# Experts in chunks of 1024 columns, with a branch on TensorE by an expert's token count

## The chip, the cores and the metric

One NeuronCore of a Trainium2 chip runs the whole kernel. The metric is the device time of one execution in microseconds, as a median of several runs. TensorE (PE) multiplies matrices, VectorE (DVE) and ScalarE (ACT) work elementwise, GpSimd (POOL) does little here, and SyncE (SP) issues the loads of the weights from HBM.

## The reference

A trunk of two layers over 256 tokens with 1024 features, in float32. Layer 0 is attention and a dense SwiGLU, layer 1 a gated recurrence (HGRN2) and eight SwiGLU experts, of which each token uses two. The change lies in the experts alone:

```python
def moe_swiglu(u, w_router, w_gate, w_up, w_down):      # D 1024, 8 experts, D_FF_EXPERT 3584
    t = u.reshape(B * S, D)                             # 256 tokens
    logits = (t @ w_router).astype(F32)
    top_vals, top_idx = lax.top_k(logits, 2)
    top_w = jax.nn.softmax(top_vals, axis=-1)
    gates = jnp.sum(jax.nn.one_hot(top_idx, N_EXPERTS) * top_w[..., None], axis=1)
    for e in range(N_EXPERTS):
        y = swiglu(t, w_gate[e], w_up[e], w_down[e])    # (silu(t @ wg) * (t @ wu)) @ wd
        out = out + gates[:, e:e + 1] * y
```

With the inputs of this reference the numbers of tokens of experts 0 to 7 are 65, 69, 45, 58, 68, 76, 61 and 70 (worked out from the reference on a CPU; the second and third highest logits of a token are nowhere closer than 0.015).

## The kernel before

**Exact products in three passes.** Weights and rows are float32. `split` cuts each weight tile into two parts: ACT copies it to `w_hi` in float32r (the format that PE multiplies at full rate), and DVE subtracts that from the raw tile and writes the rest to `w_lo`. Rows are cut in the same way (`xgh` and `xgl`, or `hh` and `hl`). `mm3` (lines 100 to 103) then adds three products in one PSUM bank: high rows by `w_hi`, high rows by `w_lo`, low rows by `w_hi`. The rows are the stationary operand (`lhsT`), 512 weight columns stream.

**Experts.** Each expert has 128 slots for its tokens. `route` works out the votes (`sel`), each token's place in an expert's list (`place`) and its gate (`gw`); `one_hot` makes from `place` a matrix of tokens by slots, and `gather_pair` multiplies the tokens by it, for two experts at once (256 columns). `Job` is a chunk of 512 of an expert's 3584 hidden columns, seven to an expert: `gate` and `up` (two loads of 1 MB each, four conversions and four subtractions of 128x1024 each, 24 products each), `turn` (four transposes of `hm`, then `hh` and `hl`) and `down` (again 1 MB twice, 24 products, into two banks `py` that live over the expert). `run_jobs` puts the gate of the next chunk ahead of `turn`, and `up` ahead of `down`. After an expert's last chunk `scatter` multiplies `py` by the turned one-hot matrix, and DVE adds the result, times the gate, to the residual stream `h`. The first gate (`FirstJob.gate`) works on all 256 tokens, 48 products, so that PE has work while the tokens are routed.

**Order and queues.** SP's queue holds the loads in program order; each lands in one of `NRAW` = 14 buffers `raws` of 8 KB per partition, freed when DVE has subtracted. `w_hi` and `w_lo` have four buffers each (`subs`). The tile framework orders each engine's instructions; an instruction waits on semaphores for what it reads and for its buffer. At the end `values_load` reads the greatest token count into a register of each engine (line 1261), and a branch (line 1262) leaves out a block for slots 128 to 255, which these inputs don't need.

Of the kernel before, what the change touches and what calls it, by code (L numbers as in the profile page):

```python
# [8 lines left out]
F32 = mybir.dt.float32  # L9
# [17 lines left out]
NRAW = 14  # L27
NSUB = 4
STOP = None
# [10 lines left out]
def tile_trunk(  # L40
# [25 lines left out]
    subs = ctx.enter_context(tc.tile_pool(name="subs", bufs=NSUB))  # L66
# [3 lines left out]
    early = ExitStack()  # L70
    xts = early.enter_context(tc.tile_pool(name="xts", bufs=1))
# [62 lines left out]
    def col_steps(xh, xl, w, c0, ps):  # L134
        """steps, one per k-tile, of x @ w[:, c0:c0+256] into ps, token tile after token tile"""
# [15 lines left out]
    def row_steps(xh, xl, wv, ks, acc, first, last):  # L151
        """steps, one per k-tile and token tile, of x @ w (all 1024 columns) into acc[t][c]"""
# [13 lines left out]
    def row_tail(xh, xl, wv, k0, acc, last, kx=0, first=False, between=None):  # L166
        """two k-tiles of x @ w, token tile by token tile"""
# [11 lines left out]
    def weave(fill, main):  # L179
        """the steps of fill, with those of main after the given amounts of fill"""  # L180
# [12 lines left out]
    def table_fn(*a, **k):  # L193
        """an activation that needs its table: those keep their order"""
# [9 lines left out]
    def gain_tile(g, late):  # L204
        """a norm's gains on all partitions; loaded once the given 1 / rms is known"""
# [13 lines left out]
    GAIN_A = 32     # columns of the first norm's gains  # L219
# [11 lines left out]
    def turn_params(rows):  # L231
        """gains and lower-bound logits to columns"""
# [4 lines left out]
    def small_params(lam_in):  # L237
        """factors into the gains; lambda of the differential attention, negated, on every partition"""
# [15 lines left out]
    def root(ap):  # L254
        """ap ** -0.5: from its logarithm, then one step of Newton's to full accuracy"""
# [9 lines left out]
    def rsqrt_mean(ap, n, width):  # L265
        """(ap / n + eps) ** -0.5"""
# [3 lines left out]
    def rms(t):  # L270
        """1 / rms of the rows of h[t], the sum taken by halves"""
# [31 lines left out]
    def norm_T(hgs, gain, acc, into=None):  # L303
        """(h * gain)^T in two parts, and 1 / rms of the rows of h; after h += acc"""
# [775 lines left out]
    class Job:  # L1080
# [6 lines left out]
        def rows(self):  # L1087
            return [(*self.shared["xg"], self.es)]
# [247 lines left out]
```

## Time and profile before

| what | value |
|---|---|
| time, median of 3 runs | 1511.85 us (1510.98 to 1514.09) |
| span of the profiled execution | 1509.5 us |
| median less that span | 2.35 us |
| PE, DVE, ACT busy | 98%, 82%, 69% |
| HBM read | 427.41 MB |

The profiled execution's time is its span; what the runs' median has more lies around the span or is the difference of one execution from another. Busy shares are those of the whole span. The experts take it from about 495 us to 1503 us, and before that lie the layers that the change leaves alone.

### The profile page before, as it was taken

What the parts mean: (1) busy time and instruction counts of PE and PEld (TensorE: products, weight loads), DVE (VectorE), ACT (ScalarE), POOL (GpSimd) and SP (SyncE); (2) the same over time, 40 slices, a digit from 0 to 9 for tenths busy, and PEclk for the clock granted to TensorE, in tenths of its full rate; (3) what the DMA queues carried; (4) which work ended last, traced back from release to release, by engine and by line L of the source; (5) the groups of instructions that cost most, each with busy time, mean ns of one, the idle gap of its engine ahead of it and who ended that gap; (6) DMA issues with size and microseconds to landing.
All of it is one profiled execution on the core that took longest, in us unless ns stands there. A gap on an engine that the chain in (4) does not pass through costs nothing.

```text
span 1509.5 us, 20242 instructions
## 1 busy us (share of the span) xinstructions
PE 1476.0 (98%) x7573; PEld 1228.3 (81%) x7573; DVE 1243.6 (82%) x1474; ACT 1042.5 (69%) x1293; POOL 14.9 (1%) x32
## 2 busy tenths in 40 slices
PE   7999999999999999999999999999999999999997
PEld 6787899998888788888888878888777887887885
DVE  7775655566767899999899998898889889889886
ACT  6655544445656788878778877777777777777774
POOL 1000000000000000000000000000000000000000
PEclk9999999999999999999999999999999999999999
DMA  9933456555443499999999999999999999999970
GB/s 312 368 117 112 137 185 195 178 185 182 140 156 125 142 376 363 373 364 362 360 325 377 377 329 362 371 315 362 362 369 345 361 355 326 362 363 343 365 260 31
DMA packets 208683, 429.85 MB, mean 285 GB/s; under 512 B 7290, under 2 KB 58530, under 8 KB 208578
## 3 DMA queue, kind: packets, MB, share of 16 engines
q1 hardware_dynamic: 208082, 426.82, 80.2%
q0 software_dynamic: 496, 1.67, 0.4%
q8 instruction: 61, 1.00, 0.3%
q14 instruction: 44, 0.36, 0.1%
HBM read 427.41 MB, written 1.05 MB: 284 GB/s over the span
## 4 chain that ended last, share of the span: by engine, by line
PE 92%; DVE 3%; ACT 2%; issue 1%; DMA 1%; POOL 0%; SPq 0%; ACTq 0%; DVEq 0%; POOLq 0%
PE acc L102 17%; PE acc L101 17%; PE acc L103 16%; PE pj L103 8%; PE pj L102 8%; PE pj L101 8%; PE pj L342 3%; PE pj L344 3%; PE pj L343 3%; DVE w_lo L91 2%; PE tp L1116 1%; PE pj L759 1%; PE pj L760 1%; PE pj L761 1%; PE acc L1069 1%
## 5 line engine op out<-in xcount | busy, mean ns | idle before, releaser
L91 DVE TENSOR_TENSOR w_lo<-raw,w_hi 128x1024 fp32r<-128x1024 f32 x810 | 958.5, 1221 | 163.4 <-ACT w_hi L91 146.1
L91 ACT ACTIVATE w_hi<-raw 128x1024 fp32r<-128x1024 f32 x810 | 835.8, 1058 | 275.8 <-PE acc L103 101.9
L102 PE MATMUL acc<-w_lo,xgh 128*128 128x512 f32 x904 | 357.2, 395 | 0.9
L101 PE MATMUL acc<-w_hi,xgh 128*128 128x512 f32 x904 | 355.9, 394 | 1.0 <-ACT xgh L294 1.0
L103 PE MATMUL acc<-w_hi,xgl 128*128 128x512 f32 x904 | 353.1, 391 | 0.0
L102 PEld LDWEIGHTS acc<-w_lo,xgh 128*128 128x128 f32 x904 | 169.7, 188 | 50.3 <-DVE w_lo L91 14.5
L101 PEld LDWEIGHTS acc<-w_hi,xgh 128*128 128x128 f32 x904 | 169.8, 188 | 36.4 <-ACT xgh L294 1.2
L103 PEld LDWEIGHTS acc<-w_hi,xgl 128*128 128x128 f32 x904 | 169.7, 188 | 33.8
L102 PE MATMUL pj<-w_lo,hh 128*128 128x512 f32 x448 | 177.1, 395 | 0.3
L103 PE MATMUL pj<-w_hi,hl 128*128 128x512 f32 x448 | 174.6, 391 | 0.3
L101 PE MATMUL pj<-w_hi,hh 128*128 128x512 f32 x448 | 161.1, 391 | 2.2 <-ACT hh L1120 1.7
L101 PEld LDWEIGHTS pj<-w_hi,hh 128*128 128x128 f32 x448 | 84.1, 188 | 21.5 <-ACT hh L1120 2.7
L102 PEld LDWEIGHTS pj<-w_lo,hh 128*128 128x128 f32 x448 | 84.1, 188 | 18.2 <-DVE w_lo L91 1.6
L103 PEld LDWEIGHTS pj<-w_hi,hl 128*128 128x128 f32 x448 | 84.1, 188 | 17.5 <-DVE hl L1121 1.1
L342 PE MATMUL pj<-xh,w_hi 128*128 128x256 f32 x320 | 90.8, 284 | 0.6 <-DVE hm L676 0.6
L344 PE MATMUL pj<-xh,w_lo 128*128 128x256 f32 x320 | 90.6, 283 | 0.0
L343 PE MATMUL pj<-xl,w_hi 128*128 128x256 f32 x320 | 90.6, 283 | 0.0
L1106 ACT ACTIVATE sg<-acc 128x512 f32<-128x512 f32 x55 | 33.0, 599 | 46.7 <-PE acc L103 46.7
L342 PEld LDWEIGHTS pj<-xh,w_hi 128*128 128x128 f32 x320 | 61.4, 192 | 1.2 <-DVE hm L676 0.8
L343 PEld LDWEIGHTS pj<-xl,w_hi 128*128 128x128 f32 x320 | 61.4, 192 | 0.4
L344 PEld LDWEIGHTS pj<-xh,w_lo 128*128 128x128 f32 x320 | 61.4, 192 | 0.0
L1120 ACT ACTIVATE hh<-tp 128x512 fp32r<-128x512 f32 x56 | 33.3, 595 | 40.4 <-PE pj L102 33.2
(296 smaller groups left out, 1648.1 us busy)
## 6 DMA issues: line engine op xcount, KB each, us to landing
raw<-in_moe_w_gate_dram SPq DMA_DIRECT2D x112, 1024.0 KB, 7.1
raw<-in_moe_w_up_dram SPq DMA_DIRECT2D x112, 1024.0 KB, 7.6
raw<-in_moe_w_down_dram SPq DMA_DIRECT2D x110, 1024.0 KB, 7.4
raw<-in_ffn_w_gate_dram SPq DMA_DIRECT2D x22, 512.0 KB, 4.0
raw<-in_ffn_w_up_dram SPq DMA_DIRECT2D x22, 512.0 KB, 5.1
raw<-in_ffn_w_down_dram SPq DMA_DIRECT2D x11, 1024.0 KB, 4.9
raw<-in_hgrn_w_in_dram SPq DMA_DIRECT2D x10, 1024.0 KB, 5.7
raw<-in_attn_w_in_dram SPq DMA_DIRECT2D x16, 512.0 KB, 9.1
```

The source lines that it names most:

```text
L91: split.last = nc.scalar.activation(hi, view, AF.Copy), nc.vector.tensor_sub(lo, view, f32(hi))
L101: nc.tensor.matmul(ps, lhsT=xh, rhs=wh, start=first, stop=False, skip_group_check=chk)
L102: nc.tensor.matmul(ps, lhsT=xh, rhs=wl, start=False, stop=False, skip_group_check=chk)
L103: nc.tensor.matmul(ps, lhsT=xl, rhs=wh, start=False, stop=last, skip_group_check=chk)
L342: nc.tensor.matmul(o, lhsT=wh[:, i, j], rhs=xh[:, k], start=k == 0 and j == 0, stop=False, skip_group_check=True)
L343: nc.tensor.matmul(o, lhsT=wh[:, i, j], rhs=xl[:, k], start=False, stop=False, skip_group_check=True)
L344: nc.tensor.matmul(o, lhsT=wl[:, i, j], rhs=xh[:, k], start=False, stop=k == KT - 1, skip_group_check=True)
L759: nc.tensor.matmul(o, lhsT=wh[:, k], rhs=xh[:, k], start=first, stop=False, skip_group_check=True)
L760: nc.tensor.matmul(o, lhsT=wh[:, k], rhs=xl[:, k], start=False, stop=False, skip_group_check=True)
L761: nc.tensor.matmul(o, lhsT=wl[:, k], rhs=xh[:, k], start=False, stop=last, skip_group_check=True)
L1106: nc.scalar.activation(self.sg, ps, AF.Silu)
L1120: nc.scalar.activation(self.hh, ptv, AF.Copy)
```

## The change

The experts' code is written anew. These are its parts:

- A chunk has 1024 columns (the first of expert 0 and the last of every other have 512), and a chunk's weights come in `Group`s of one 1 MB load, one conversion and one subtraction of 128x2048. `w_hi` has three such buffers and `w_lo` two. `NRAW` is 11. A row of a load is 4 KB (gate, up) or 8 KB (down), where it was 2 KB or 4 KB.
- `route` also counts the tokens of each expert, and `value_load` reads the eight counts into registers of PE.
- Every group's products stand in a branch on PE. Above 64 tokens: the same 12 products. Up to 64 tokens: 8 products, whose stationary operand has 64 high rows and 64 low rows at once (the high and low part of a row lie side by side in `xg` and `hq`, and a slice with step 2 takes 64 of each). Rows 64 to 127 of the result are then the low rows' share.
- Behind a gate or an up of any expert ACT copies the bank to `low`. In `fold`, in a second branch on PE, experts of up to 64 tokens add rows 64 to 127 to rows 0 to 63 with a product by `lower`; the other experts jump over it.
- For experts of up to 64 tokens the one-hot matrices are other ones (`pick`, `even`, `twice`), and the transposes in `turn` multiply by a permutation `order`. The sharing of low rows on the way out is done by `scatter`, whose one-hot matrix has each token twice.

```diff
-NRAW = 14
+NRAW = 11
@@ route
+            if t == NT - 1:
+                pc = bank("tp")
+                for u in range(NT):
+                    nc.tensor.matmul(pc[:, 0:NE], lhsT=ones, rhs=sel[:, u], start=(u == 0), stop=(u == NT - 1))
+                nc.vector.tensor_copy(count, pc[:, 0:NE])
...
+                nc.vector.tensor_scalar(few, pc[:, 0:NE], float(HS), None, op0=ALU.is_le)
...
+                nc.vector.tensor_reduce(out=cmax_i, in_=count, axis=AX.X, op=ALU.max)
@@ Group
+        def split(self):
+            self.hi = parts.tile([P, 2048], F32R, name="w_hi", tag="w_hi", bufs=3)
+            self.lo = parts.tile([P, 2048], F32R, name="w_lo", tag="w_lo", bufs=2)
+            nc.scalar.activation(self.hi, self.raw, AF.Copy)
+            nc.vector.tensor_sub(self.lo, self.raw, f32(self.hi))
+        def __call__(self):
+            if self.n is None:
+                return self.arm(self.hi, self.lo, True)
+            with tc.If(self.n > HS) as cmp:
+                self.arm(self.hi, self.lo, True)
+            with cmp.Else():
+                self.arm(self.hi, self.lo, False)
...
+    def products(xq, wh, wl, ps, large, first, last):
+        if large:
+            xh, xl = xq[:, 0], xq[:, 1]
+            mm(ps, (xh, xh, xl), (wh, wl, wh), first, last)
+        else:
+            xs = xq.rearrange("p q s -> p (q s)")[:, 0:2 * P:2]
+            mm(ps, (xs, xs), (wh, wl), first, last)
@@ Job
+        def low(self, box):
...
+            for lo, ps in zip(box["low"], box["ps"]):
+                nc.scalar.activation(lo, ps, AF.Copy)
+        def fold(self, box):
...
+            with tc.If(self.n < HS + 1):
+                for lo, ps in zip(box["low"], box["ps"]):
+                    nc.tensor.matmul(ps, lhsT=lower, rhs=lo, start=False, stop=True, skip_group_check=True)
...
-                nc.tensor.transpose(out=pt[:, i * P:(i + 1) * P], in_=self.hm[:, i * P:(i + 1) * P], identity=ident)
+                    nc.tensor.transpose(out=pt[:, i * P:(i + 1) * P], in_=self.hm[:, b, i // 2, i % 2],
+                                        identity=self.shared.get(("order", self.e), ident))
@@ the jobs
-        for ch in range(NCH):
+        widths = (1, 2, 2, 2) if e == 0 else (2, 2, 2, 1)
+    numbers = [nc.tensor.value_load(count[0:1, e:e + 1], min_val=0, max_val=S) for e in range(NE)] if TWO else [None] * NE
```

**PE where a gate's products end.** In these rows of PE's program the columns are line, operation and operands, and what an instruction waits for on semaphores. First the last products of an up (`acc`) of the kernel before, and behind them the transposes of the chunk's `hm`:

```order
L101 MATMUL acc<-w_hi,xgh 128x512 [waits Activation_49]
L102 MATMUL acc<-w_lo,xgh 128x512 [waits DVE_49]
L103 MATMUL acc<-w_hi,xgl 128x512
L101 MATMUL acc<-w_hi,xgh 128x512
L102 MATMUL acc<-w_lo,xgh 128x512
L103 MATMUL acc<-w_hi,xgl 128x512
L1116 MATMUL tp<-ident,hm 128x128 [waits PE_49]
L1116 MATMUL tp<-ident,hm 128x128 x3
```

The same engine in the changed kernel, from the last products of a group for small experts to the next group; L1133 is the branch of a group, L1216 that of `fold`, and L1140 a product (`xg` holds both parts of the rows):

```order
L1133 UNCONDITIONAL_BRANCH
L1140 MATMUL acc<-w_hi,xg 128x512 [waits Activation_49]
L1140 MATMUL acc<-w_lo,xg 128x512 [waits DVE_49]
L1133 UNCONDITIONAL_BRANCH
L1216 COMPARE_AND_BRANCH
L1218 MATMUL acc<-low,lower 128x512 [waits Activation_49] x2
L1216 UNCONDITIONAL_BRANCH
L1216 UNCONDITIONAL_BRANCH [waits PE_49]
L1133 COMPARE_AND_BRANCH
L1140 MATMUL acc<-w_hi,xg 128x512 [waits Activation_49]
L1140 MATMUL acc<-w_lo,xg 128x512 [waits DVE_49]
```

A branch now stands ahead of each group, and a second one ahead of `fold`'s two products; the path that jumps over them ends in a branch of L1216 that waits on PE's own semaphore, ahead of the next group. The instruction that waits there is a semaphore wait for all products issued before it.

**PE while the tokens are routed.** Before, rows of the first gate (`acc`, lines 101 to 103) stand around the two small products that count a token's place (`tp<-sel`), all ahead of the gathers:

```order
L103 MATMUL acc<-w_hi,xgl 128x512
L101 MATMUL acc<-w_hi,xgh 128x512
L102 MATMUL acc<-w_lo,xgh 128x512
L1036 MATMUL tp<-sel,up 128x8 [waits DVE_49,PE_49,Pool_49]
L1036 MATMUL tp<-sel,ones 128x8
L103 MATMUL acc<-w_hi,xgl 128x512
L101 MATMUL acc<-w_hi,xgh 128x512
L102 MATMUL acc<-w_lo,xgh 128x512
L103 MATMUL acc<-w_hi,xgl 128x512
```

Changed, where L1065 is the new count over the experts, L1060 the place, L1140 the first gate (`both` holds all tokens' rows), and L1406 the loads of the counts into PE's registers:

```order
L1065 MATMUL tp<-sel,ones 128x8 [waits DVE_49]
L1140 MATMUL acc<-w_hi,both 128x512
L1060 MATMUL tp<-sel,up 128x8 [waits DVE_49]
L1065 MATMUL tp<-sel,ones 128x8
L1140 MATMUL acc<-w_hi,both 128x512
L1140 MATMUL acc<-w_lo,both 128x512
L1406 TENSOR_LOAD count [waits DVE_49,Activation_49,Pool_49]
L1406 ISA x2
L1406 TENSOR_LOAD count
L1406 ISA x2
```

Of the 48 products of the first gate 11 now stand ahead of the eight loads (two more instructions, register work, behind each), and 37 behind them; before, all 48 stood ahead of the gathers with no load among them.

**DVE within an expert.** Before, a `w_lo` subtraction has 1024 columns, and the chunk's other two instructions (`hm` at L1111, `hl` at L1121) stand between them:

```order
L1121 TENSOR_TENSOR hl<-tp,hh 128x512
L91 TENSOR_TENSOR w_lo<-raw,w_hi 128x1024 x4
L1111 TENSOR_TENSOR hm<-acc,sg 128x512
L91 TENSOR_TENSOR w_lo<-raw,w_hi 128x1024 x8
L1121 TENSOR_TENSOR hl<-tp,hh 128x512
```

Changed (L1201 is `hm`, L1229 the low half of `hq`):

```order
L1128 TENSOR_TENSOR w_lo<-raw,w_hi 128x2048
L1216 UNCONDITIONAL_BRANCH
L1201 TENSOR_TENSOR hm<-acc,sg 128x2x128x2
L1133 UNCONDITIONAL_BRANCH
L1128 TENSOR_TENSOR w_lo<-raw,w_hi 128x2048
L1201 TENSOR_TENSOR hm<-acc,sg 128x2x128x2
L1133 UNCONDITIONAL_BRANCH
L1128 TENSOR_TENSOR w_lo<-raw,w_hi 128x2048
L1229 TENSOR_TENSOR hq<-tp,hq 128x4x128
L1133 UNCONDITIONAL_BRANCH
L1128 TENSOR_TENSOR w_lo<-raw,w_hi 128x2048
```

Half as many subtractions of twice the width stand there, and a branch of L1133 for each group and of L1216 for each fold, since a branch on the count is passed by all engines.

## Rows read from the trace of the kernel before

**Rows 1.** The profile page of the whole execution: its span, the busy time of each engine, and the share of each engine in the chain of work that ended last.
```profile
span 1509.5 us, 20242 instructions
PE 1476.0 (98%) x7573; PEld 1228.3 (81%) x7573; DVE 1243.6 (82%) x1474; ACT 1042.5 (69%) x1293; POOL 14.9 (1%) x32
...
PE 92%; DVE 3%; ACT 2%; issue 1%; DMA 1%; POOL 0%; SPq 0%; ACTq 0%; DVEq 0%; POOLq 0%
```

**Rows 2.** Busy time of each engine in two stretches of the experts' stage: the stretch (us), then PE, PEld, DVE, ACT and POOL (instructions in brackets); the last three columns are granted clock, DMA share and GB/s.
```profile
560.00:700.00 140.00, 140.00 (x637) 115.62 (x636) 131.31 (x121) 112.72 (x119) 0.00 (x0) 1.00 1.01 368
...
900.00:1100.00 200.00, 199.35 (x905) 161.69 (x904) 178.61 (x171) 151.12 (x165) 0.00 (x0) 1.00 0.98 355
```

**Rows 3.** Groups of instructions by line in the experts' stage (520 to 1505 us): busy time, mean ns of one, idle time of the engine just before them and what ended it.
```profile
L91 DVE TENSOR_TENSOR w_lo<-raw,w_hi 128x1024 fp32r<-128x1024 f32 x664 | 780.3, 1221 | 57.0 <-ACT w_hi L91 41.6
L91 ACT ACTIVATE w_hi<-raw 128x1024 fp32r<-128x1024 f32 x664 | 681.6, 1059 | 123.6 <-PE acc L103 56.4 <-PE pj L103 54.8 <-DVE w_lo L91 11.2
L1121 DVE TENSOR_TENSOR hl<-tp,hh 128x512 fp32r<-128x512 f32 x56 | 38.7, 691 | 12.4 <-ACT hh L1120 12.4
L1111 DVE TENSOR_TENSOR hm<-acc,sg 128x512 f32<-128x512 f32 x56 | 38.6, 689 | 19.9 <-PE acc L103 19.6
L1120 ACT ACTIVATE hh<-tp 128x512 fp32r<-128x512 f32 x56 | 33.3, 595 | 40.4 <-PE pj L102 33.2 <-PE tp L1116 7.2
L1204 DVE SCALAR_TENSOR_TENSOR h<-tp,gw,h 128x512 f32<-128x512 f32 x32 | 22.5, 745 | 3.2 <-PE tp L1203 3.1
L102 PEld LDWEIGHTS acc<-w_lo,xgh 128*128 128x128 f32 x885 | 166.2, 188 | 49.7 <-DVE w_lo L91 14.5
```

**Rows 4.** Instructions in order of time inside the experts' stage: start, duration, what. The first and the last of 13 products of 512 columns that follow each other on PE, the four transposes of a chunk and the product behind them, two rows of gathers (four products of 256 columns each), and four subtractions that follow each other on DVE.
```profile
559.69 0.39 PE L103 MATMUL acc<-w_hi,xgl 128*128 128x512 f32 x1
...
562.41 0.40 PE L103 MATMUL acc<-w_hi,xgl 128*128 128x512 f32 x1
562.65 0.60 PE L1116 MATMUL tp<-ident,hm 128*128 128x128 f32 x4
...
563.32 0.40 PE L102 MATMUL acc<-w_lo,xgh 128*128 128x512 f32 x1
...
740.50 4.92 DVE L91 TENSOR_TENSOR w_lo<-raw,w_hi 128x1024 fp32r<-128x1024 f32 x4
...
744.74 0.64 PE L1069 MATMUL acc<-oneh,nl 128*128 128x256 f32 x4
...
745.22 0.64 PE L1069 MATMUL acc<-oneh,nh 128*128 128x256 f32 x4
```

**Rows 5.** One line's instructions, `back` of `back_to_tokens`, which marks the end of experts 1, 3 and 5 (from three stretches; the two start times are equal as there is one instruction in each).
```profile
L1187 ACT ACTIVATE back<-tp x1: 378/378/378, 749.2 to 749.2; 128x256 fp32r<-128x256 f32 x1
...
L1187 ACT ACTIVATE back<-tp x1: 393/393/393, 997.4 to 997.4; 128x256 fp32r<-128x256 f32 x1
...
L1187 ACT ACTIVATE back<-tp x1: 393/393/393, 1247.0 to 1247.0; 128x256 fp32r<-128x256 f32 x1
```

**Rows 6.** Who SyncE, which issues the weight loads, waited for (total us, times, longest).
```profile
SPq L85 <- DVE w_lo L91: 1170.2, 380, 17.1
```

**Rows 7.** One of the stretches of 10 us in the experts' stage with the highest rate of the weight loads (columns as in the windows above).
```profile
540.00:550.00 10.00, 10.00 (x48) 8.26 (x47) 8.91 (x9) 8.29 (x10) 0.00 (x0) 1.00 1.04 394
```

**Rows 8.** Sequencer instructions at the end of the program (lines 1261 and 1262: a value loaded into a register of every engine, then a branch over the block of slots 128 to 255, which is not entered): count, duration in ns (least, median, most), first and last start.
```profile
L1261 PEldq TENSOR_LOAD <-cmax_i x1: 803/803/803, 1503.4 to 1503.4; - x1
L1261 SPq FUSED_REGOPS  x1: 186/186/186, 1504.2 to 1504.2; - x1
L1262 ACTq COMPARE_BRANCH  x1: 50/50/50, 1504.2 to 1504.2; - x1
L1262 PEldq COMPARE_BRANCH  x1: 4108/4108/4108, 1504.3 to 1504.3; - x1
L1262 DVEq COMPARE_BRANCH  x1: 76/76/76, 1504.3 to 1504.3; - x1
L1262 DVEq EVENT_SEMAPHORE  x1: 21/21/21, 1504.9 to 1504.9; - x1
L1262 ACTq EVENT_SEMAPHORE  x1: 17/17/17, 1507.2 to 1507.2; - x1
L1262 PEldq EVENT_SEMAPHORE  x1: 51/51/51, 1508.5 to 1508.5; - x1
```

**Rows 9.** The chain of work that ended last, in order of time, at a place where PE had waited for a conversion: start, length, what.
```profile
1492.02 1.07 ACT w_hi L91
1493.08 0.04 issue
1493.13 0.50 PE pj L101
1493.63 0.23 PE pj L103
```

**Rows 10.** Instructions in order of time at the entry of the experts' stage: the place of the second token tile's tokens (`place`), the last product of the first gate and the first gather, and the first product behind the gathers.
```profile
510.98 0.17 DVE L1037 SCALAR_TENSOR_TENSOR place<-tp,sel 128x8 f32<-128x8 f32 x1 [0.70 <-PE tp L1036]
...
512.27 0.39 PE L103 MATMUL acc<-w_hi,xgl 128*128 128x512 f32 x1
512.50 0.63 PE L1069 MATMUL acc<-oneh,nh 128*128 128x256 f32 x4
...
518.12 0.40 PE L101 MATMUL acc<-w_hi,xgh 128*128 128x512 f32 x1
```

More of the change, by code (lines that the diff above doesn't have):

```diff
@@ new lines, in __init__, with xq, into, begin @@
+            self.first, self.last = c0 == 0, c0 + nb * 512 == FE
+        def xq(self, k):
+            return self.shared["xg"][:, k, self.e]
+        def into(self, w, box):
+            nk, nb, width = 4 // self.nb, self.nb, self.nb * 512
+            def begin():
+                box["ps"] = [bank("acc", 4) for _ in range(nb)]
+            def group(k0):
+                def arm(hi, lo, large):
+                    for j in range(nk):
+                        for b in range(nb):
+                            cs = slice(j * width + b * 512, j * width + b * 512 + 512)
+                            products(self.xq(k0 + j), hi[:, cs], lo[:, cs], box["ps"][b], large, k0 + j == 0, k0 + j == KT - 1)
+                return Group(lambda r: [(r.rearrange("p (k c) -> p k c", k=nk), w[:, k0:k0 + nk, self.c0:self.c0 + width])],
+                             arm, self.n)
+            return [begin] + [group(k0) for k0 in range(0, KT, nk)] + [lambda: self.low(box)]
@@ new lines, in down, with begin, group, arm @@
+        def down(self):
+            sh = self.shared
+            py = "py", self.e
+            def begin():
+                if self.first:
+                    sh[py] = [bank("pj") for _ in range(2)]
+            def group(a):
+                def arm(hi, lo, large):
+                    for i in range(2):
+                        for c in range(2):
+                            cs = slice(i * D + c * 512, i * D + c * 512 + 512)
+                            products(self.hq[:, a // 2, a % 2 * 2 + i], hi[:, cs], lo[:, cs], sh[py][c], large,
+                                     self.first and a == 0 and i == 0, self.last and a == 2 * self.nb - 1 and i == 1)
+                return Group(lambda r: [(r, self.wd[:, self.c0 // 256 + a, :])], arm, self.n)
+            return [begin] + [group(a) for a in range(2 * self.nb)] + ([self.out] if self.last else [])
@@ L1139, in tile_trunk, with out @@
+        def out(self):
+            sh = self.shared
+            back = back_to_tokens(self.oneh(sh))
+            for c in range(2):
+                scatter(c, sh["py", self.e][c], back, self.gates(sh))
     class LastJob(Job):
@@ new lines, in group, with arm @@
+            def group(c):
+                def arm(hi, lo, large):
+                    for j in range(4):
+                        cs = slice(j * 512, (j + 1) * 512)
+                        products(self.hq[:, 0, j], hi[:, cs], lo[:, cs], sh["py", self.e][c], large, False, j == 3)
+                wd = self.wd.rearrange("p r (i c) -> p r i c", i=2)
+                return Group(lambda r: [(r[:, a * D:(a + 1) * D].rearrange("p (i c) -> p i c", i=2),
+                                         wd[:, self.c0 // 256 + a, :, HALF[c]]) for a in range(2)], arm, self.n)
@@ L1152, in tile_trunk, with before, after @@
+            def before():
+                box["back"] = back_to_tokens(self.oneh(sh))
+            def after(c):
+                scatter(c, sh["py", self.e][c], box["back"], self.gates(sh), put)
+            return [before, group(0), lambda: after(0), group(1), lambda: after(1)]
     class FirstJob(Job):
         def gate(self):
-            self.ch_rows = [(*dense, TOK[t]) for t in range(NT)]
-            self.sgh = lows.tile([P, NT, 512], F32R, name="sgh", tag="low1")
-            self.sgl = []
@@ L1169, in up, with gated @@
+            return [begin] + [group(k0) for k0 in (0, 4)] + [end]
+        def gated(self):
+            pass
         def up(self):
             sh = self.shared
[L1171 to L1177 removed]
@@ new lines, in pick, with fn @@
+    def pick(e, sh):
+        def fn():
+            sh["pick"] = one_hot(e, even, "low")
+            sh["oneh"] = one_hot(e, twice, "oneh")
+            for i in range(2):
+                at = small.tile([P, 1], F32, name="at", tag="at")
+                nc.vector.scalar_tensor_tensor(at, step, few[:, e + i:e + i + 1], place1, op0=ALU.mult, op1=ALU.add)
+                sh["order", i] = moe.tile([P, P], F32, name="order", tag="order", bufs=3)
+                nc.vector.tensor_scalar(sh["order", i], slot1, at, None, op0=ALU.is_equal)
+        return fn
```

319 lines of the change are left out of this document (175 added, 144 removed).

## The prediction

> **What bounds the kernel now.** The first view is the page: PE is busy 98% of the span, DVE 82%, ACT 69%, and 92% of the chain that ended last is PE's [rows 1]. Then the windows, since the experts fill two thirds of the span and the shares of the whole say little of them: from 560 to 700 us PE is busy 140.00 of 140.00 us and from 900 to 1100 us 199.35 of 200.00, at a granted clock of 1.00, while DVE stands at 0.94 and 0.89 [rows 2]. So PE is the bound and DVE a near second. The ends of experts 1, 3 and 5 lie at 749.2, 997.4 and 1247.0 us [rows 5], so two experts take 248.2 and 249.6, or 124.5 us for one.
>
> Does PE's own work explain that? Thirteen products that follow each other start 2.72 us apart in all, so one costs 0.2267 us and a group of 12 costs 2.72 [rows 4]. An expert has 42 loads of 1 MB and so 504 products: 114.3 us. Its transposes cost 7 x 0.46 (562.41 to 563.32, less two products), its half of a pair's 64 gather products 32 x 0.118 (four start 0.47 us apart), its scatter about 2: together 9. That is 123.4 of 124.5.
>
> The weights are not late: SP waited 1170.2 us for buffers that DVE frees [rows 6]. An expert is 44.04 MB, 354 GB/s at the present pace; a busy stretch shows 394 [rows 7], which would be 112 us an expert. That is the floor of the loads as far as the rows show it.
>
> **What the change saves.** With up to 64 tokens 8 products replace 12. By the counts only experts 2, 3 and 6 are in that arm; the other five keep all 12. A small expert's PE time falls to 76.2 + 14 folds of 0.23 + 9 = 88 us, so DVE sets the pace. A subtraction of 1024 columns takes 1.23 us back to back (4.92 for four) [rows 4], one of 512 columns 0.691 [rows 3]; the slope, 1.035 ns a column, gives 2.29 for 2048. Then 42 x 2.29 = 96.2 us; `hm` and `hl`, 14 x 0.69 = 9.7; the scatter, 4 x 0.745 [rows 3] and two more of 0.69 = 4.4; casts of gathered rows (two of 0.69) and the one-hot matrices, by estimate, about 3: 113.4 us. ACT stays below: 42 conversions of 2.0 (1.059, plus 1024 columns at the slope to `hh`'s 0.595), and 8.4 for the new copies `low`, about 105. DVE does not run without gaps: where a group's buffer is the second of only two, the next subtraction waits for PE to end the group before, and a chain gate, `hm`, transposes, `hl` stands at each chunk. I put 4.5 us on that, 118 us an expert. The saving is 6.5 us, times three **-19.5 us**; the bounds are 113.4 (**-33**) and 122 (**-8**).
>
> **What it costs on PE: the folds.** For the five large experts nothing is saved, and each gate and up gets a second branch. The path around `fold` waits until all products before it are done, and only then may PE's sequencer pass on the next group. In the kernel before, the next group's products are in the queue while the last ones run: products start 0.2267 apart though each lasts 0.39 [rows 4], so 0.16 us overlap that a drain gives back. After it come the semaphore (0.02 to 0.05; the instruction itself 0.051) and the next group's comparison (0.05 to 0.08 on ACT and DVE) [rows 8]. Where PE resumes after a wait, the first product takes 0.50 instead of 0.23 until the next one starts [rows 9], 0.27 more. The sum is 0.16 + 0.09 + 0.10 + 0.27 = 0.62 us. There are 7 such folds in expert 0 (its first gate has none) and 8 in each of the other four: 39, **+24 us**. [...] From below, if the restart comes without the long first product, 0.21 and +8; from above, if the jump costs the 0.45 us that DVE shows from comparison to next instruction (1504.3 + 0.08 to 1504.9) [rows 8], 1.07 and +42. The small experts' 24 folds stand in slack of PE.
>
> **The branches of the groups** stand ahead of each load's products, 210 of them in the large experts. PE's row is the worst one: 4108 ns for one comparison, where ACT shows 50 and DVE 76 [rows 8]. That one jumps over a whole expert's code; the new ones pass 8 or 12 products. I take the near kind. A large group's sequencer work is 24 instructions of about 0.06 (half of 0.118, at which gather products are passed on [rows 4]) = 1.42, plus 0.45 and 0.08, in 2.72 us of products. So the branches lie behind PE's queue: 0. If that cover were gone, 210 x 0.5 = +105 us.
>
> On DVE each group has a jump too. Large experts leave it 124.5 - 113.4 = 11 us, or 0.26 per group; jumps of 0.05 to 0.08 use 2 to 4 of that. With two `w_lo` buffers in place of four there is less to even out a late `hm`. I put **+2 us** on it (0 to 10).
>
> **What it costs at the entry.** Before, PE's 48 products of the first gate all lie in the time in which the tokens are routed; the last starts at 512.27, the gathers start at 512.50 and the products behind them at 518.12 [rows 10]. Now 11 stand ahead of the eight loads of counts and 37 behind. The count is there when the second tile's `place` is, 510.98 + 0.17, plus a product and a cast, about 512. A load takes 0.803 on PE, and the register work behind it 0.186 and more [rows 8]: 1.05 each, 8.4 us, till 520.4, with PE idle. Then 37 x 0.2267 = 8.4, 528.8; then the gathers, 5.6, 534.5. That is **+16.5 us**. Without the register work, and with the loads 1.5 us earlier, +12; if the loads overlap by half, +9. From above +22, if PE then waits for the first gate's activations as well, which were 6 us ahead of their use before.
>
> **Smaller parts.** The greatest count is ready long before the end, which takes a product, a reduction and a cast off the tail, ahead of the register load at 1503.4 [rows 8]: by estimate **-1 us** (0 to -1.5). Rows of 4 and 8 KB, and 11 buffers instead of 14, change nothing while SP waits for buffers: 11 MB are still 32 us ahead at 354 GB/s.
>
> **The sum.** -19.5 + 24 + 2 + 16.5 - 1 = +22. The profiled span is 1509.5 and the runs' median 2.35 more: **1534 us**.
>
> **The rivals.**
> - **The loads' pace, not DVE's.** If DVE runs without the gaps I put in and the larger rows raise the rate, a small expert takes 109 us. Three save 46; against costs of 42, 1507. The point from which it is faster is 110.8 us a small expert. For it: SP's 1170 us of waits. Against: DVE's own sum is 113.4 [rows 3, 4], and 109 needs subtractions of 2.19. To the same side leads a cheap entry (+9) with cheap folds (+8), at any pace of DVE.
> - **PE passes the folds quickly**, at 0.21 us each: 1534 - 16 = 1518. For it: a product 0.04 us after what it waited for [rows 9]. Against: the 0.50 right behind it.
> - **Jumps miss.** PE's experts' code is larger by the second arms. If 28 jumps, some one in seven of the large experts' groups, take PE's 4.1 us [rows 8] less 1.2 us of queued products, 28 x 2.9 = 80: 1614. [...] Jumps of 0.45 that DVE can't hide would do as much: (42 + 8) x 0.45 = 22, on 113.4, is 136 an expert. Against: DVE passes its far jump in half a microsecond.
> - **The stationary operand with step 2 loads slowly.** A load of weights reads 188 ns [rows 3] and hides behind products. At twice that, not hidden, 8 of them make 3.0 us a small group and 139 us an expert: 3 x 21 more, 1599. No row shows such a load.
> - **Nothing happens**, as the branch costs and saves little everywhere: needs an entry at 0, against which rows 10 speak.
>
> **How the numbers follow.** Forecast 0.56 (1515 to 1556 by the bounds of folds, DVE and entry); loads' pace 0.13 (1507, from 1496 to 1512); quick folds 0.15 (1518, with an entry of +9 1510); missing jumps 0.10; slow operand 0.06. The range of 8 in 10 leaves out the two slow rivals and the outer ends of the first: 1502 to 1572. The measurement tells about 0.2%, 3 us, from no change. Faster (below 1509) is most of the loads' pace and a third of the quick folds, with a cheap entry beside them: 0.16; within 0.2% 0.08; slower 0.76.
>
> **What would show it.** In the profile after: PE busy near 100% and 12 products in 2.72 us in large experts, with a gap of about 0.6 us behind every fold; 3 experts of about 118 us with PE below 80% and DVE above 95%; the gathers of the first pair ending at about 534 instead of 518. The forecast is wrong if PE's branches show microseconds, if DVE's 2048-column subtraction is not 2.29, or if the first gate's products come ahead of the loads.

## The result, and the profile after

The changed kernel takes 1533.91 us (median of 4 runs, 1532.71 to 1534.31) against 1511.41 for the kernel before on the same chip: a ratio of 1.0149 (1.0135 to 1.0164). The prediction was 1534. Its profiled execution has a span of 1532.5 us, 23.0 more than before.

The page after: span, the engines, and the groups of the new conversion (ACT), the new subtraction (DVE) and `hm` (DVE), with busy time, mean ns, idle time before them and what ended it.
```profile
span 1532.5 us, 19486 instructions
PE 1428.2 (93%) x7111; PEld 1150.3 (75%) x7111; DVE 1241.6 (81%) x1189; ACT 1044.2 (68%) x1068; POOL 15.7 (1%) x34
...
L1128 DVE TENSOR_TENSOR w_lo<-raw,w_hi 128x2048 fp32r<-128x2048 f32 x336 | 762.9, 2286 | 87.7 <-PE acc L1140 47.2
L1127 ACT ACTIVATE w_hi<-raw 128x2048 fp32r<-128x2048 f32 x336 | 640.0, 1918 | 147.8 <-PE pj L1140 62.8
...
L1201 DVE TENSOR_TENSOR hm<-acc,sg 128x512 f32<-128x512 f32 x56 | 60.5, 1100 | 9.4 <-PEq L1216 8.6
```
PE has 462 products fewer than in [rows 1] and 48 us less busy time, and yet the span is longer: it was shortened where PE was cut and lengthened elsewhere. DVE's busy time has hardly moved (1243.6 to 1241.6), since one subtraction of 2048 columns (2286 ns) saves little on two of 1024 (2 x 1221 [rows 3]), and `hm` now takes 1100 ns instead of 689 [rows 3].

The windows after, columns as in [rows 2]: two pieces of the entry, a stretch of the small experts 2 and 3, one of the large experts 4 and 5.
```profile
506.00:512.00 6.00, 4.50 (x14) 3.78 (x15) 5.05 (x15) 0.30 (x2) 0.00 (x0) 0.50 0.59 195
516.00:522.00 6.00, 3.38 (x8) 2.71 (x9) 1.19 (x6) 0.00 (x0) 0.00 (x0) 0.50 0.00 0
...
910.00:1005.00 95.00, 83.62 (x343) 62.00 (x343) 92.94 (x59) 79.32 (x63) 0.00 (x0) 0.98 1.01 395
1020.00:1120.00 100.00, 96.54 (x417) 75.48 (x416) 86.73 (x51) 74.81 (x59) 0.00 (x0) 1.00 0.95 344
```
In the small experts DVE is busy 92.94 of 95 us and the loads run at 395 GB/s, which is the rate of [rows 7]: the bound has moved from PE to DVE, with the loads close behind. SyncE waited 77.1 us of these 95 for buffers that DVE frees, and no engine waited for a load. In the large ones PE is busy 96.54 of 100, where it was 199.35 of 200 [rows 2]. At the entry the granted clock is 0.50 in both pieces; PE had stood idle for 3.92 and for 5.52 us (below). The kernel before has 1.00 from 505 to 512.

What an expert costs is read from the trace as the time from the first subtraction of its first group to that of the next expert (the last one ends where its last product starts), in us; "start" is when expert 0's comes; 2, 3 and 6 are the small ones. The other rows are experiments from below.

| kernel | start | 0 | 1 | 2 small | 3 small | 4 | 5 | 6 small | 7 |
|---|---|---|---|---|---|---|---|---|---|
| before | 487.0 | 140.0 | 125.1 | 119.2 | 128.5 | 122.7 | 126.9 | 122.8 | 126.8 |
| after | 505.2 | 147.4 | 133.5 | 113.1 | 114.9 | 128.0 | 133.4 | 112.5 | 134.5 |
| no branch (e1) | 506.1 | 136.2 | 128.8 | 126.3 | 131.1 | 126.9 | 131.0 | 126.9 | 132.8 |
| no branch, aligned (e10) | 506.5 | 133.8 | 126.4 | 124.2 | 129.1 | 125.0 | 128.9 | 124.9 | 130.6 |
| aligned (e9) | 508.1 | 144.8 | 131.1 | 112.9 | 114.0 | 125.7 | 131.0 | 111.7 | 132.1 |
| fold in the arm (e3) | 505.4 | 148.0 | 132.4 | 115.7 | 115.6 | 128.4 | 132.2 | 112.7 | 135.0 |

The small experts give back 6.1 + 13.6 + 10.3 = 30.0 us. Experts 4 and 5 take 261.4 instead of 249.6, 5.9 more each. Expert 0 begins 18.1 later and takes 7.3 more.

**The entry.** PE after, in order of time (start, duration, what, and in brackets the idle time ahead with what ended it): the first product of `w_lo`, the last one ahead of the loads of counts, the first behind them, the first gather.
```profile
507.50 0.79 PE L1140 MATMUL acc<-w_lo,both 128*128 128x512 f32 x1 [3.92 <-DVE w_lo L1128]
...
512.72 0.39 PE L1140 MATMUL acc<-w_lo,both 128*128 128x512 f32 x1
518.62 1.22 PE L1140 MATMUL acc<-w_hi,both 128*128 128x512 f32 x2 [5.52 <-issue]
...
529.05 0.64 PE L1107 MATMUL acc<-low,nh 128*128 128x256 f32 x4
```
The loads themselves, line 1406: count, least, median and most ns, first and last start.
```profile
L1406 PEldq TENSOR_LOAD <-count x8: 299/301/493, 512.9 to 517.9; - x8
L1406 PEldq FUSED_REGOPS  x8: 146/146/160, 513.5 to 518.3; - x8
```
The gathers start at 529.05 where 512.50 stood before [rows 10]. The loads are part of it with 5.52 us, 0.69 each. The rest is a wait of 3.92 us for the first subtraction, and products at a granted clock of 0.50 on either side.

That subtraction is late rather than long. The first row is the kernel before; the others are the changed kernel, where the first group's conversion (ACT) is done at 496.1 and its subtraction comes 9 us after that:
```profile
487.05 2.35 DVE L91 TENSOR_TENSOR w_lo<-raw,w_hi 128x1024 fp32r<-128x1024 f32 x2
...
494.19 1.91 ACT L1127 ACTIVATE w_hi<-raw 128x2048 fp32r<-128x2048 f32 x1 [1.32 <-issue]
...
505.17 2.27 DVE L1128 TENSOR_TENSOR w_lo<-raw,w_hi 128x2048 fp32r<-128x2048 f32 x1
```
Between these two moments DVE works on the tokens' rows and on the routing. No run tries another order there.

**Inside a large expert.** PE after in expert 0: three products of `w_lo`, one in every three products, and a fold's place between two groups.
```profile
561.26 0.39 PE L1140 MATMUL acc<-w_lo,xg 128*128 128x512 f32 x1
...
561.96 0.39 PE L1140 MATMUL acc<-w_lo,xg 128*128 128x512 f32 x1
...
562.66 0.39 PE L1140 MATMUL acc<-w_lo,xg 128*128 128x512 f32 x1
...
567.80 0.40 PE L1140 MATMUL pj<-w_hi,hq 128*128 128x512 f32 x1
568.51 0.49 PE L1140 MATMUL pj<-w_hi,hq 128*128 128x512 f32 x1 [0.32 <-PEq L1216]
568.84 0.39 PE L1140 MATMUL pj<-w_lo,hq 128*128 128x512 f32 x1
```
Three products take 0.70 us, 0.2333 each, at a granted clock of 1.00; before, 0.2267 [rows 4]. That is the unforeseen part. What is called the full rate of `float32r` above was measured as that 0.2267, 0.44 ns a column; four float32 products of 256 columns in the attention of the kernel before (L512, from 133.79 to 134.85) took 1.06 us, 1.04 ns a column. Behind the fold's branch the next product comes 0.71 after the last one and its follower 0.33 later, instead of 0.233 twice: a gap of 0.48 + 0.10 = 0.57 us.

The branches on PE's sequencer, that of the groups (L1133) and that of the folds (L1216) with its semaphore, and what PE waited for (us in total, times, longest).
```profile
L1133 PEldq COMPARE_BRANCH  x542: 65/169/441, 533.4 to 1517.9; - x181
...
L1216 PEldq COMPARE_BRANCH  x87: 72/179/288, 540.6 to 1500.0; - x87
L1216 PEldq EVENT_SEMAPHORE  x39: 51/51/51, 543.4 to 1503.3; - x39
```
```profile
PE acc L1140 <- DVE w_lo L1128: 36.6, 41, 3.9
PE pj L1140 <- DVE w_lo L1128: 8.6, 15, 0.7
PE pj L1140 <- PEq L1216: 6.6, 19, 0.5
PE acc L1140 <- PEq L1216: 6.4, 20, 0.4
```
None of the new branches took a microsecond (at most 0.441 us), and none of the groups' branches appears among PE's waits. The 39 folds that large experts pass over appear with 19 + 20 waits, as counted.

### The profile page after: what moved, and what is told of

It reads as the page before. It is cut to its first block, busy times and chain, and to the rows that moved or that the text cites. A ratio compares the mean times of both kernels' runs of the same rounds, so it can differ in the third digit from the quotient of the medians.

```text
span 1532.5 us, 19486 instructions
## 1 busy us (share of the span) xinstructions
PE 1428.2 (93%) x7111; PEld 1150.3 (75%) x7111; DVE 1241.6 (81%) x1189; ACT 1044.2 (68%) x1068; POOL 15.7 (1%) x34
## 5 line engine op out<-in xcount | busy, mean ns | idle before, releaser
L1128 DVE TENSOR_TENSOR w_lo<-raw,w_hi 128x2048 fp32r<-128x2048 f32 x336 | 762.9, 2286 | 87.7 <-PE acc L1140 47.2
L1127 ACT ACTIVATE w_hi<-raw 128x2048 fp32r<-128x2048 f32 x336 | 640.0, 1918 | 147.8 <-PE pj L1140 62.8
L1140 PE MATMUL acc<-w_hi,xg 128*128 128x512 f32 x1440 | 493.1, 398 | 6.4 <-PEq L1216 6.4
L1140 PE MATMUL acc<-w_lo,xg 128*128 128x512 f32 x888 | 361.5, 407 | 35.4 <-DVE w_lo L1128 32.7
L1140 PEld LDWEIGHTS acc<-w_hi,xg 128*128 128x128 f32 x1440 | 273.8, 190 | 73.2 <-ACT w_hi L1127 14.9
L1140 PE MATMUL pj<-w_hi,hq 128*128 128x512 f32 x728 | 259.5, 404 | 8.9 <-PEq L1216 6.6
L92 DVE TENSOR_TENSOR w_lo<-raw,w_hi 128x1024 fp32r<-128x1024 f32 x138 | 168.6, 1223 | 103.5 <-ACT w_hi L92 100.4
L1140 PEld LDWEIGHTS acc<-w_lo,xg 128*128 128x128 f32 x888 | 170.3, 192 | 103.0 <-DVE w_lo L1128 69.6
L92 ACT ACTIVATE w_hi<-raw 128x1024 fp32r<-128x1024 f32 x138 | 145.7, 1058 | 143.5 <-PE pj L344 71.3
L1140 PE MATMUL pj<-w_lo,hq 128*128 128x512 f32 x448 | 181.1, 404 | 9.6 <-DVE w_lo L1128 8.6
L1140 PEld LDWEIGHTS pj<-w_hi,hq 128*128 128x128 f32 x728 | 139.0, 191 | 46.0 <-ACT w_hi L1127 12.9
L1140 PEld LDWEIGHTS pj<-w_lo,hq 128*128 128x128 f32 x448 | 85.8, 192 | 36.6 <-DVE w_lo L1128 20.7
L1201 DVE TENSOR_TENSOR hm<-acc,sg 128x512 f32<-128x512 f32 x56 | 60.5, 1100 | 9.4 <-PEq L1216 8.6
```

Of the source, the lines that this page charges most:

```text
L92: split.last = nc.scalar.activation(hi, view, AF.Copy), nc.vector.tensor_sub(lo, view, f32(hi))
L1127: nc.scalar.activation(self.hi, self.raw, AF.Copy)
L1128: nc.vector.tensor_sub(self.lo, self.raw, f32(self.hi))
L1140: nc.tensor.matmul(ps, lhsT=x_, rhs=w_, start=first and i == 0, stop=last and i == len(xs) - 1, skip_group_check=True)
L1201: nc.vector.tensor_mul(self.hm[:, b].rearrange("s a i p -> s a p i"), self.pu["ps"][b].rearrange("s (a p i) -> s a p i", a=2, i=2), self.s ...
```

## The experiments

Each ratio is to runs of the kernel before on the same chip (medians of 1511.4 to 1511.54 us). Pads are tiles that shift what is allocated behind them and are not read.

**e1: is the pace of 0.2333 the branches' doing?** All experts run the large arm, without loads of counts, folds or branches; groups, buffers and places stay.
```diff
-TWO = True
+TWO = False
```


> The changed kernel with the flag TWO off: chunks and groups as changed, but no counts, no branches, no folds and no copies low; all eight experts take 12 products a group. In the trace of the changed kernel products of large experts start 0.2333 us apart instead of 0.2267. Theory A, the slower pace belongs to the new groups (buffers, layout) and not to the branches: 8 experts x 504 x 0.0067 = 27 us over the kernel before, and the entry keeps the 4 us in which PE waits for the first wide subtraction: 1540 to 1545 us, pace 0.233. Theory B, the pace comes with the branches: pace 0.227 and 1512 to 1518 us.


Measured: 1557.82 us, 1.0311 (1.0294 to 1.0329), and three products still take 0.70. So the pace is not the branches', and the groups without the arms cost 46 us. PE at the entry of e1: the first product of `w_lo` and the first gather.
```profile
508.41 0.79 PE L1140 MATMUL acc<-w_lo,both 128*128 128x512 f32 x1 [3.92 <-DVE w_lo L1128]
...
524.52 0.64 PE L1107 MATMUL acc<-low,nh 128*128 128x256 f32 x4
```
Without a single load of counts the gathers are already 12.0 us later than before. PE waits 3.92 us for the first subtraction, which comes at 506.1 here, and from 507 to 517 the granted clock is 0.51.

**e2: do the places of the buffers set the pace?** The pool of `w_hi` and `w_lo` is opened ahead of the others.
```diff
+    parts = ctx.enter_context(tc.tile_pool(name="parts", bufs=1))
     xgs = ctx.enter_context(tc.tile_pool(name="xgs", bufs=1))
...
-    parts = ctx.enter_context(tc.tile_pool(name="parts", bufs=1))
```


> The changed kernel with the pool of w_hi and w_lo opened ahead of the other pools of the experts' stage, so that these tiles lie at the lower addresses (122464 up) where the kernel before has its weight tiles and rows, and the rows above them; nothing else. Theory A, the address of the streamed operand sets the pace of 0.2333 us: it returns to 0.2267, five large experts gain 3.4 us each, 1517 us. Theory B, the address doesn't matter: 0.2333 and 1534 us.


Measured: 1525.33, 1.0091 (1.0074 to 1.0107), 8.6 us faster than the changed kernel. Gate and up run at 0.2274 to 0.228 a product, down still at 0.233. The pace goes with addresses, and `xg` and `hq` are touched differently.

**e3: what do the folds cost?** Where the next group is the same expert's, the fold's products move to the end of a small arm that is there anyway, and 34 of the 39 passed-over branches vanish.
```diff
             with cmp.Else():
                 self.arm(self.hi, self.lo, False)
+                if self.post:
+                    self.post()
```


> The changed kernel with fold's products put at the end of the small arm of the group that precedes them, wherever that group is the same expert's: 34 of the 39 folds that large experts jump over are gone, with the wait for all earlier products. Theory A, a jumped fold costs a large expert about 0.57 us (0.71 us between two products instead of 0.233, and 0.33 to the one after): 34 x 0.57 = 19 us, 1514 us. Theory B, most of the loss in large experts is the slower product pace and the drains cost 0.2 each: 1527 us.


Measured: 1538.88, 1.0183 (1.0166 to 1.02), slower by 5. What PE waited for in e3:
```profile
PE acc L1142 <- DVE w_lo L1128: 35.8, 38, 3.9
PE tp L1234 <- DVE hm L1206: 16.8, 30, 1.4
...
PE pj L1142 <- DVE w_lo L1128: 10.5, 18, 1.5
```
The waits at the 34 folds are gone, and `tp` waits 16.8 us for `hm` where it waited 1.9 in the changed kernel. The edit moves more than the branch: inside experts 4 and 5 `hm` of an up now starts 15.4 us after the copies `low`, where it started 2.35 after them, since the group that the fold is put into comes that much later. Experts 4 and 5 take 260.6 instead of 261.4, and PE's waits in them add up to 8.8 us where they were 8.5. So e3 shows what this edit is worth, and not the price of a gap by itself.

**e4: is it the loads' place?** The loads of counts stand behind the first gate, among the first pair's gathers (from 525.3 to 536.2 us).
```diff
+                numbers.extend(nc.tensor.value_load(count[0:1, e:e + 1], min_val=0, max_val=S) for e in range(NE))
...
-    numbers = [nc.tensor.value_load(count[0:1, e:e + 1], min_val=0, max_val=S) for e in range(NE)] if TWO else [None] * NE
+    numbers = []
```


> The changed kernel with the eight loads of counts behind the first gate and among the first gathers, not ahead of the gate's last 37 products. Theory A, the loads stop PE (5.5 us without a product, from 513.1 to 518.6, and a granted clock of 0.5 in 6.8 us behind it): 6 to 9 us less, 1525 to 1528 us. Theory B, the entry is long because PE waits for the first wide subtraction and the one-hot matrices anyway: 1533 us.


Measured: 1530.59 (1527.99 to 1535.27), 1.012 (1.0103 to 1.0137): 3.3 us less by the medians, but its four runs spread over 7.3 us and the traced one is the slowest of them, so the gain is not clear of the spread. The first gather comes at 527.54 instead of 529.05, and the loads, now beside queued products, leave 1.13 us of idle time on PE instead of 5.52. The rest of these 4.4 us is not seen at the gather: from 512 to 521 PE is busy 9.00 of 9.00 us, at a granted clock of 0.50, so the products in the loads' place start about 0.43 us apart.

**e5 and e6: which addresses?** e5 pads the changed kernel (twice 96 bytes) so that weights, `xg` and `hq` begin at equal places modulo 128 bytes; e6 shifts the activations of the kernel before by 64 bytes and changes nothing else (its diff).
```diff
+    pad1 = ctx.enter_context(tc.tile_pool(name="pad1", bufs=1))
+    nc.vector.memset(pad1.tile([P, 16], F32, name="pad1"), 0.0)
     xgs = ctx.enter_context(tc.tile_pool(name="xgs", bufs=1))
```


> The changed kernel with two unused tiles of 96 bytes a partition, one ahead of the pool moe and one ahead of the pool parts, so that the rows (xg, hq) and the weights (w_hi, w_lo) begin at the same remainder modulo 128 bytes (96). In the changed kernel xg begins at 96, hq at 0 and the weights at 32; in the run with the weight tiles at the low addresses xg and the weights at 96, and gate and up ran at 0.227 us, but hq at 0 and down at 0.233. Theory A, the pace depends on whether the two operands of a product agree modulo 128 bytes: all products of large experts at 0.227, 5 x 3.4 = 17 us less at most, 1517 to 1522 us. Theory B, it depends on the region of the addresses, which doesn't change here: 0.233 and 1534 us.

> The kernel before with one unused tile of 64 bytes a partition ahead of the pool xgs, so that the experts' rows (xgh, xgl, hh, hl) move by 64 bytes against the weights; nothing else. Theory A, agreement modulo 128 bytes: products of the experts at 0.233 instead of 0.227, 4032 x 0.0067 = 27 us more, 1538 us. Theory B: 0.227 and 1511.5 us.


Measured: e5 1529.93, 1.0129 (1.0111 to 1.0146), with products of `xg` at 0.2325 and of `hq` at 0.2285 to 0.2297. e6 1531.83, 1.0136 (1.0119 to 1.0153): 64 bytes cost the kernel before 20.4 us. Its products of PE, four in a row:
```profile
599.69 0.39 PE L101 MATMUL acc<-w_hi,xgh 128*128 128x512 f32 x1
599.92 0.40 PE L102 MATMUL acc<-w_lo,xgh 128*128 128x512 f32 x1
600.16 0.39 PE L103 MATMUL acc<-w_hi,xgl 128*128 128x512 f32 x1
600.39 0.40 PE L101 MATMUL acc<-w_hi,xgh 128*128 128x512 f32 x1
```
0.70 us for three, with the old groups, the old order and no branch. 128 bytes aren't the period: in e5 the weights lie 384 bytes behind `xg` modulo 512 and 256 behind `hq`, both multiples of 128, and the two paces differ.

**e7 and e8: a third buffer for `w_lo`,** paid with one of the raw ones; e8 adds e5's pads and e4's late loads.
```diff
-NRAW = 11
+NRAW = 10
...
-            self.lo = parts.tile([P, 2048], F32R, name="w_lo", tag="w_lo", bufs=2)
+            self.lo = parts.tile([P, 2048], F32R, name="w_lo", tag="w_lo", bufs=3)
```


> The changed kernel with three w_lo buffers instead of two and 10 raw buffers instead of 11. Theory A, two w_lo buffers tie DVE to PE (DVE stood 68 us idle on PE's products and folds, PE 45 us on w_lo): small experts go from 113 to the 111 that DVE has to do, large ones lose up to 3 us of waits, 10 to 20 us less in all, 1514 to 1524 us. Theory B, the waits only move elsewhere: 1531 to 1535 us.

> The changed kernel with the two pads, three w_lo buffers (10 raw buffers) and the eight loads of counts behind the first gate; folds as changed. If the three act each on their own: 1534 less 3 (loads), less 12 to 17 (pace), less 10 (buffers): 1504 to 1509 us, at or below the kernel before. If DVE takes over as the bound in large experts too: 1512 to 1518 us.


Measured: e7 1563.95, 1.0343 (1.0325 to 1.036), 30 us slower than the changed kernel; e8 1550.22, 1.0265 (1.0248 to 1.0282). No expectation held either. What ACT waited for in e7:
```profile
ACT hq L1228 <- PE tp L1225: 53.3, 10, 9.3
```
In the changed kernel that line reads 25.5 us in 12 waits, at most 3.2. But with the new count of buffers the scheduler also put ACT's and DVE's instructions in another order, so the buffer alone was not measured. What the 30 us come from stays open.

**e9 to e12: equal places modulo 512 bytes.** e9 is the changed kernel with all three at 96 modulo 512; e10 the same without branches, as e1; e11 the kernel before with its activations 512 bytes on; e12 is e9 with e3's fold and e4's loads.
```diff
+    nc.vector.memset(pad1.tile([P, 120], F32, name="pad1"), 0.0)
...
+    nc.vector.memset(pad2.tile([P, 88], F32, name="pad2"), 0.0)
```


> The changed kernel with unused tiles of 480 and 352 bytes a partition ahead of the pools moe and parts, so that rows (xg, hq) and weights begin at the same remainder modulo 512 bytes (96). So far products ran at 0.227 us where the two operands differ by 0 modulo 512 bytes, at 0.2285 to 0.2297 where by 256, 0.2325 by 384 and 0.2333 by 64, 192 or 160. Theory A, modulo 512: 0.227 in gate, up and down of large experts; with gate and up alone at that pace it was 8.6 us less, so 12 to 13 us less here, 1521 us. Theory B, the run with the low addresses was fast for another reason: 0.23 and 1528 us or more.

> The changed kernel with the flag TWO off (no counts, branches, folds or copies low; all experts large) and the pads of 480 and 352 bytes. It was 1557.8 us without the pads. Theory A, the groups of 1 MB lose against the kernel before by their pace and their entry alone: 8 x 504 x 0.0065 = 26 us less, 1532 us. Theory B, with the pace back DVE's w_lo waits take over: 1540 us or more.

> The kernel before with one unused tile of 512 bytes a partition ahead of the pool xgs (64 bytes there cost 20 us and brought the pace of 0.233). Theory A, modulo 512: rows and weights agree again, 0.227 and 1511.5 us. Theory B, any move of the rows against the weights, or the memset itself, costs: 1525 us or more.

> The changed kernel with the pads of 480 and 352 bytes, the loads of counts behind the first gate, and the folds in the small arms. Theory A, the three add up as they measured alone (12 less, 3 less, 5 more): 1524 us. Theory B, with the faster pace the folds' gaps of 0.48 us are no longer slack of DVE and their removal pays 3 us in each large expert: 1505 to 1510 us, below the kernel before.


Measured:

| kernel | us | ratio to before |
|---|---|---|
| e9 | 1523.23 | 1.0069 (1.0053 to 1.0086) |
| e10 | 1539.85 | 1.0182 (1.0165 to 1.0199) |
| e11 | 1512.25 | 1.0003 (0.9993 to 1.0013) |
| e12 | 1523.68 | 1.0074 (1.0057 to 1.0091) |

PE in e9, a product of `w_lo` in every three, and a fold:
```profile
1059.82 0.39 PE L1144 MATMUL acc<-w_lo,xg 128*128 128x512 f32 x1
...
1060.50 0.39 PE L1144 MATMUL acc<-w_lo,xg 128*128 128x512 f32 x1
...
1061.18 0.39 PE L1144 MATMUL acc<-w_lo,xg 128*128 128x512 f32 x1
...
1064.81 0.39 PE L1144 MATMUL pj<-w_hi,hq 128*128 128x512 f32 x1
1065.51 0.49 PE L1144 MATMUL pj<-w_hi,hq 128*128 128x512 f32 x1 [0.32 <-PEq L1220]
```
0.68 for three: the old pace is back, and 10.7 us with it; the gap at the fold has stayed. e11 keeps time and pace (0.23, 0.22, 0.23 from product to product), so 64 bytes cost time and 512 do not. e12 joins what helped or was meant to help and is no better than e9. No run was faster than the kernel before.

What PE waited for in e10, experts 4 and 5:
```profile
PE acc L1144 <- DVE w_lo L1132: 5.7, 6, 1.0
```
What DVE waited for in them, as far as PE ended the wait:
```profile
DVE w_lo L1132 <- PE pj L1144: 5.8, 11, 0.9
DVE w_lo L1132 <- PE acc L1144: 4.7, 11, 1.1
```
The kernel before has none of these waits in these two experts. DVE waits until PE has read a `w_lo` buffer, and PE then waits for the next subtraction. This is the price of larger groups with two `w_lo` buffers, seen apart from pace and branches; no run tells the groups' size from the count of buffers.

**The chain of runs,** each by medians: the new groups alone, at the old pace, +28.4 (e10); the pace +18.0 (e1 less e10); the branches with their small arms -23.9 (the changed kernel less e1). Together +22.5. The sizes hold for this order of steps: with the branches in place the pace is worth 10.7 (e9), not 18.0.

## Why the prediction was right, point by point

The number was right, and the signs and places of its terms too. The sizes were not, and they cancelled: that the forecast lies within a microsecond of the result is luck. From the table of experts and the span:

| term | forecast | measured |
|---|---|---|
| three small experts | -19.5 | -30.0 |
| five large experts (folds 24, DVE 2) | +26 | +29.5 (5 x 5.9, from experts 4 and 5) |
| entry and the ends | +15.5 | +23.5 (what is left of 23.0) |
| sum | +22 | +23.0 |

- **Small experts: the bound was right, DVE's own work was mis-sized.** An expert takes 113.1, 114.9 and 112.5 us, forecast 118: 113.4 of work and 4.5 of gaps. These are the windows of experts 2, 3 and 6 (columns as in [rows 2]), and three subtractions in a row:
```profile
785.99:899.05 113.06, 97.97 (x395) 71.26 (x394) 109.42 (x69) 93.88 (x74) 0.00 (x0) 1.00 0.98 377
899.05:1013.96 114.91, 102.33 (x428) 76.38 (x427) 112.50 (x73) 95.08 (x78) 0.00 (x0) 0.99 1.01 397
1275.40:1387.87 112.47, 99.03 (x397) 72.78 (x396) 108.30 (x63) 93.11 (x73) 0.00 (x0) 0.98 0.98 376
...
899.06 6.68 DVE L1128 TENSOR_TENSOR w_lo<-raw,w_hi 128x2048 fp32r<-128x2048 f32 x3
```
DVE is busy 110.1 us on average and idle 3.4. So the gaps were nearly as forecast, and the term that failed is DVE's sum, 3.3 too high. One subtraction takes 2.286 us, forecast 2.29, but in a row they start 2.20 apart; against that `hm` takes 1.10, not 0.69. That work and gaps together come out at the 113.4 of the bound is chance. The three took 123.5 us on average before, not 124.5, which is why the gain is 30 and not the 33 of that bound. PE, forecast at 88 us and below 80%, is busy 98 to 102 us, 87 to 89%. The loads' pace, the rival to the faster side, needed 110.8 us an expert and did not come.
- **Folds: the gap is as forecast, the cost is not.** 0.57 us behind each, forecast 0.62. But experts 4 and 5 with branches take 261.4 where e1 takes 257.9, and 256.7 (e9) where e10 takes 253.9: 2.8 to 3.5 us for 16 folds, about 0.2 each, or 8 for all 39. That is the lower bound of the term, and it includes the groups' branches. What PE waited for in experts 4 and 5 of e9:
```profile
PE acc L1144 <- DVE w_lo L1132: 3.0, 4, 1.2
PE pj L1144 <- PEq L1220: 2.9, 8, 0.5
PE acc L1144 <- PEq L1220: 2.5, 8, 0.3
```
The folds bring 5.4 us of waits, and the wait for `w_lo` falls from 5.7 (e10) to 3.0, which leaves 2.7 of the 2.8 us. So the likeliest reading is that PE would have waited for `w_lo` anyway, and that a gap fills time in which DVE catches up. The step that failed is to add each gap whole to the time. In the prediction's own sum two numbers don't follow from their rows: the comparison stands at about 0.10 where its rows say 0.05 to 0.08, and without the long first product 0.35 is left, +14, not 0.21 and +8. No run shows the 0.10 by itself; after the change the records of L1216 on PE read 0.072 to 0.288 us, 0.179 in the middle, over comparisons and jumps together. The rival of quick folds names the right price with a wrong reason, as PE does not pass them quickly (a gap of 0.57 us, against its 0.21).
- **DVE with two buffers: too small by a factor of five.** Forecast +2 in all; e10 against the kernel before gives 4.3 us for experts 4 and 5, 2.1 each, so 10.7 for five, just past the upper bound. PE's waits for `w_lo`, 5.7 us in these two, and DVE's for PE, 10.5, name the place.
- **The pace of the products was taken as fixed, and was not.** 0.2267 became 0.2333, and the 12 products of a group took 2.80 us where 2.72 were forecast. In experts 4 and 5 that is 4.0 to 4.7 us (e1 less e10, the changed kernel less e9), about 2 each. The prediction has no term for it; the folds' surplus paid for it. Along the chain of runs the 5.9 of a large expert are then 2.1 for groups, 2.0 for the pace and 1.8 for branches and folds.
- **The entry: the time was right, its makeup wrong.** The gathers were forecast at 528.8 and start at 529.05. The loads were to take 8.4 and take 5.5; the 0.803 of [rows 8] is a load by itself (0.556 at the end of the changed kernel, L1434), and eight in a row take 0.30 with 0.39 of other work each. What the forecast missed is the wait of 3.92 us for the first wide subtraction, which comes 18.1 us later than the first one did before, and the granted clock of 0.50. By e1 the loads answer for 4.5 us of the 16.6 (5.4, since e1 begins its first gate 0.9 later). Of the 23.5 us, 16.6 are there at the first gather; 3.0 more stand at the start of expert 1, beyond the 5.9 of a large expert, and experts 1 and 7 take 2.5 and 1.8 beyond it. What makes these was not tried. The stretch from the start of the last product to the end is 0.4 shorter (10.06 us instead of 10.48), for which -1 was forecast.
- **Branches of the groups: nothing, as forecast.** 0.065 to 0.441 us, 0.169 in the middle, over the comparisons and the jumps at the end of an arm together (542 records for 334 groups), hidden behind queued products. No branch of PE took microseconds but the far jump at the end of the program, 3.57 (L1435) where 4.11 stood before [rows 8], so the rival of missing jumps falls.
- **The stationary operand with a step** loads in 195 to 201 ns in the small experts' stretch, against 188 before [rows 3]: that rival falls too.

Left to itself the idea of the change works: the small arm turns e1 into a kernel faster by 23.9 us. What it is set on, groups of 2048 columns at these places, costs 46 (18.0 of it the places), and only three of eight experts can earn it back.

## What to carry to other kernels

When a change re-cuts the work of a stage, price the cut alone first, with the new branch off: here it cost about twice what the branch won (46 us against 23.9). A gap that the trace shows at an instruction is not its price, where another engine's wait would fill the same time (here 0.57 us of gap at about 0.2 of price); take the price from a run without it, in which nothing else moves. After moving pools, compare the start-to-start time of one often repeated instruction with the old trace (here 0.2333 against 0.2267 us) before looking for causes in the code.

## What was not expected of the hardware

In these runs PE's pace went with how the two operands' addresses stand to each other, from 0.2267 us a product to 0.2333. In products of 512 columns in fp32r, each behind a new load of its stationary operand (the activations `xgh`, `xg`, `hq`; `w_hi` and `w_lo` stream), the start-to-start time goes by the difference of the two operands' addresses within a partition, here modulo 512 bytes (streaming less loaded):

| difference | us a product | where |
|---|---|---|
| 0 | 0.2267 at best, 0.2275 to 0.2287 in the mean of experts 4 and 5 | before, e9, e10, e11 |
| 256 | 0.2285 to 0.2297 | `hq` in e5 |
| 384 | 0.2325 | `xg` in e5 |
| 448; 160 and 192 | 0.2333 | e6; `hq` and `xg` in the changed kernel |

A difference of 0 and one of 256 can't be told apart by these runs: in experts 4 and 5 the products of `hq` start 0.2287 apart in e9 (0) and 0.2291 in e5 (256). So a period of 256 bytes fits as well as one of 512. Addresses other than these were not tried, and why it is so is open. It cost 20.4 us in e6 and 10.7 in the changed kernel.

A value loaded into a register of PE took 0.30 us in a row of eight, 0.49 for the first, and where it stood by itself 0.803 before [rows 8] and 0.556 at the end of the changed kernel.
